# A two-layer decoder trunk on one core: the first embedding projection at the attention's end, squares on VectorE, weight low parts by an accumulating DMA

## The chip, the core and the metric

The kernel runs on one core of a Trainium2 chip. The metric is the device time of one execution, in microseconds (us); before the change the median of three runs is 1500.62 us (1500.09 to 1501.07). The core's engines run their own instruction queues: PE (TensorE, matrix products, with its weight loads as PEld), DVE (VectorE), ACT (ScalarE), POOL (GpSimd) and SP (SyncE, here an issuer of DMA). They meet only at semaphores: an instruction waits until the one that makes its input, or frees its buffer, is done. SBUF holds tiles of 128 partitions; PSUM takes what PE accumulates.

## The reference

512 tokens of width 1024 pass two layers: the first with differential attention, the second with retention. Each is followed by a squared-ReLU MLP and by a gated embedding.

```
for i in range(2):
    h = rms_norm(x, norm_mix[i])
    x = x + (diff_attention(h) if i % 2 == 0 else retention(h))
    h = rms_norm(x, norm_mlp[i])
    x = x + square(relu(h @ mlp_w1[i])) @ mlp_w2[i]
    gate = sigmoid(rms_norm(x, norm_pe[i]) @ pe_w_gate[i])
    x = x + gate * (p[i] @ pe_w_up[i])          # p[i]: 512 x 256
```

The product `p[i] @ pe_w_up[i]` depends on inputs alone and on nothing that the layer computes. Everything is float32.

## The kernel before

**Tiling.** Activations lie with features in partitions: x is eight tiles of 128 x 512, and so are the normalized z. A product of two float32 values is made from three matmuls of a shorter format (`mm3`, L177): each operand is split into a high part (a cast) and a low part (what the cast left off), and high x high, high x low and low x high are accumulated. Names end in h for the high and l for the low part: zh and zl, oT6h and oT6l, wh and wl.

**Weights.** The class `Weights` (L51) streams all weights in one order, in tiles of 128 x 1024 numbered from 0. For each, SP loads the raw tile (512 KB, three buffers), ACT casts it to wh (L75) and an engine subtracts to make wl (L79); wh and wl have five buffers each, so tile i reuses the buffer of tile i - 5, and tile i is prepared four tiles ahead of its use. `lo_engines` says who subtracts: DVE, and for the tiles prepared within the attention POOL and DVE by halves.

**Stages, by the span.** Attention to about 283 us, first MLP to 629, its gated embedding to about 690, retention to about 1083, second MLP to about 1430, second gated embedding to the end. In the attention, a plan of numbers (`place`) interleaves the steps of query and key projection, scores, softmax, values and the output product, and a scheduler then orders each engine's instructions by its own costs. The output product (`out_unit`) runs in groups of heads; group 2 (heads 6 and 7) is the last: for each of eight x tiles it adds the product to x (DVE, L516), then makes zh and zl for the MLP (`make_z`; ACT L159, DVE L160) and adds the squares of x to `acc` (`squares`; ACT L228, POOL L229). `acc` goes through a cast (rsm0sh), a subtraction (rsm0sl) and two matmuls against ones (rsm0p, `rs_rows`) to the row sums that the first MLP needs when its first two products are done.

**Order around the row sums.** The MLP's product functions run two output tiles side by side at the start (`tiles`, L193) and put the row sums' two matmuls (`late[0]`) at a fixed place in the second one, by default ahead of its third input tile (`late_at` 2).

**Embedding projection.** `up_unit` makes one 128 x 512 tile of `p @ pe_w_up` with six matmuls. In layer 0 it stands in the gated embedding, one tile ahead of each gate product (`begin`), with the two weight tiles `w_up0` loaded there; DVE multiplies it from PSUM. In layer 1 all eight tiles are made at the end of the retention, from two PSUM buffers (`ps_tr`), and ACT copies them to SBUF (pus, L797). PSUM has eight buffers: three `mm`, two `s`, two `tr`, one `av`.

## Time and profile before

| | |
|---|---|
| median of three runs | 1500.62 us |
| lowest, highest | 1500.09, 1501.07 us |
| the profiled execution | 1498.45 us |
| its span | 1496.6 us |
| PE busy | 98% of the span |
| DVE busy | 55% |
| ACT busy | 41% |
| POOL busy | 12% |

The profile is one execution. Its span is the time from its first to its last instruction, and 1.85 us lie around it. The page gives shares over the whole span, which averages stages with different limits; so a stage is read from windows (busy time of each engine in a stretch), and a single wait from the timeline, in which the brackets give the engine's idle time ahead of an instruction and what ended it. Matmuls overlap, so one's duration is longer than the distance to the next. The chain of waits follows the work that ended last backwards, and gives the share of each line in it.

### The profile page before, as it was taken

What the parts mean: (1) busy time and instruction counts of PE and PEld (TensorE: products, weight loads), DVE (VectorE), ACT (ScalarE), POOL (GpSimd) and SP (SyncE); (2) the same over time, 40 slices, a digit from 0 to 9 for tenths busy, and PEclk for the clock granted to TensorE, in tenths of its full rate; (3) what the DMA queues carried; (4) which work ended last, traced back from release to release, by engine and by line L of the source; (5) the groups of instructions that cost most, each with busy time, mean ns of one, the idle gap of its engine ahead of it and who ended that gap; (6) DMA issues with size and microseconds to landing.
All of it is one profiled execution on the core that took longest, in us unless ns stands there. A gap on an engine that the chain in (4) does not pass through costs nothing.

```text
span 1496.6 us, 17071 instructions
## 1 busy us (share of the span) xinstructions
PE 1470.9 (98%) x6668; PEld 1199.6 (80%) x6668; DVE 827.7 (55%) x1217; ACT 618.7 (41%) x966; POOL 183.6 (12%) x128
## 2 busy tenths in 40 slices
PE   9999999899999999999999999999999999999998
PEld 7667667688888888888888888888778888888887
DVE  7887888853434444475464564544584343434455
ACT  6666766541323224344442432433453241323332
POOL 4123223300000000311020110301220000000020
PEclk9999999999999999999999999999999999999999
DMA  6211131243333233232314233132233333333312
GB/s 234 61 57 57 57 113 57 81 116 99 98 92 95 96 99 99 85 99 93 105 51 132 64 99 106 57 127 71 71 99 99 98 94 93 96 98 99 99 57 85
DMA packets 40256, 137.90 MB, mean 92 GB/s; under 512 B 4464, under 2 KB 4976, under 8 KB 40176
## 3 DMA queue, kind: packets, MB, share of 16 engines
q1 hardware_dynamic: 40176, 136.82, 29.5%
q8 instruction: 52, 0.85, 0.2%
q14 instruction: 28, 0.23, 0.0%
HBM read 134.70 MB, written 2.10 MB: 91 GB/s over the span
## 4 chain that ended last, share of the span: by engine, by line
PE 88%; DVE 7%; ACT 2%; issue 1%; POOL 0%; DMA 0%; SPq 0%; POOLq 0%; DVEq 0%; ACTq 0%
PE py L179 8%; PE py L180 8%; PE py L181 8%; PE ph L180 8%; PE ph L181 8%; PE ph L179 8%; PE pg L181 2%; PE pg L180 2%; PE pg L179 2%; PE rv L180 2%; PE rqk L181 2%; PE rqk L180 2%; PE rv L181 2%; PE rv L179 2%; PE rqk L179 2%; PE rg L179 2%
## 5 line engine op out<-in xcount | busy, mean ns | idle before, releaser
L75 ACT CAST wh<-raw 128x1024 fp32r<-128x1024 f32 (+1 forms) x245 | 256.4, 1048 | 620.9 <-PE py L180 235.7
L79 DVE TENSOR_TENSOR wl<-raw,wh 128x1024 fp32r<-128x1024 f32 (+1 forms) x245 | 300.6, 1228 | 60.5 <-ACT wh L75 59.4
L180 PE MATMUL ph<-zl,wh 128*128 128x512 f32 x512 | 200.1, 391 | 3.5 <-DVE zl L160 3.4
L181 PE MATMUL ph<-zh,wl 128*128 128x512 f32 x512 | 199.8, 391 | 0.0
L179 PE MATMUL ph<-zh,wh 128*128 128x512 f32 x512 | 199.5, 390 | 0.1
L179 PE MATMUL py<-hh,wh 128*128 128x512 f32 x512 | 199.2, 389 | 0.0
L180 PE MATMUL py<-hl,wh 128*128 128x512 f32 x512 | 199.2, 389 | 0.0
L181 PE MATMUL py<-hh,wl 128*128 128x512 f32 x512 | 199.2, 389 | 0.0
L582 DVE TENSOR_TENSOR x<-x,py 128x512 f32<-128x512 f32 x64 | 44.0, 688 | 200.0 <-PE py L181 200.0
L572 DVE SCALAR_TENSOR_TENSOR ht<-ph,rsm 128x512 f32<-128x512 f32 x64 | 44.0, 691 | 158.8 <-PE ph L181 158.8
L180 PEld LDWEIGHTS ph<-zl,wh 128*128 128x128 f32 x512 | 96.5, 189 | 25.1 <-DVE zl L160 5.2
L179 PEld LDWEIGHTS ph<-zh,wh 128*128 128x128 f32 x512 | 96.4, 188 | 20.7 <-issue 0.5
L181 PEld LDWEIGHTS ph<-zh,wl 128*128 128x128 f32 x512 | 96.5, 189 | 20.1
L181 PEld LDWEIGHTS py<-hh,wl 128*128 128x128 f32 x512 | 96.1, 188 | 20.1
L179 PEld LDWEIGHTS py<-hh,wh 128*128 128x128 f32 x512 | 96.1, 188 | 20.0
L180 PEld LDWEIGHTS py<-hl,wh 128*128 128x128 f32 x512 | 96.1, 188 | 19.8
L229 POOL TENSOR_TENSOR acc_p<-acc_p,sq 128x512 f32<-128x512 f32 x14 | 24.2, 1727 | 673.7 <-ACT sq L228 673.7
L79 POOL TENSOR_TENSOR wl<-raw,wh 128x512 fp32r<-128x512 f32 x28 | 46.0, 1642 | 90.0 <-ACT wh L75 70.6
L179 PE MATMUL pqk<-wh,zh 128*128 128x512 f32 x128 | 53.6, 419 | 0.0
L179 PE MATMUL pg<-zh,wh 128*128 128x512 f32 (+1 forms) x136 | 51.2, 377 | 0.0
L181 PE MATMUL pg<-zh,wl 128*128 128x512 f32 (+1 forms) x136 | 51.2, 377 | 0.0
L180 PE MATMUL pg<-zl,wh 128*128 128x512 f32 (+1 forms) x136 | 51.2, 376 | 0.0
(874 smaller groups left out, 2762.9 us busy)
## 6 DMA issues: line engine op xcount, KB each, us to landing
raw<-in_w SPq DMA_DIRECT2D x128, 512.0 KB, 3.6
raw<-in_w_qk SPq DMA_DIRECT2D x16, 512.0 KB, 3.7
raw<-in_w_g SPq DMA_DIRECT2D x16, 512.0 KB, 3.6
raw<-in_w_rv SPq DMA_DIRECT2D x16, 512.0 KB, 3.7
raw<-in_w_rqk SPq DMA_DIRECT2D x16, 512.0 KB, 4.4
raw<-in_w_rg SPq DMA_DIRECT2D x16, 512.0 KB, 3.6
raw<-in_w_ro SPq DMA_DIRECT2D x16, 512.0 KB, 3.6
raw<-in_w_o SPq DMA_DIRECT2D x8, 512.0 KB, 3.6
```

What stands on the lines that cost most here:

```text
L75: nc.scalar.copy(out=hi[:, s], in_=raw[:, s])
L79: e.tensor_tensor(out=lo[:, r], in0=raw[:, r], in1=hi[:, r].bitcast(F32), op=ALU.subtract)
L179: nc.tensor.matmul(ps, a[0], b[0], start=start, stop=False)
L180: nc.tensor.matmul(ps, a[0], b[1], start=False, stop=False)
L181: nc.tensor.matmul(ps, a[1], b[0], start=False, stop=stop)
L229: nc.gpsimd.tensor_tensor(out=acc, in0=acc, in1=sq, op=ALU.add)
L572: nc.vector.scalar_tensor_tensor(out=t, in0=s[1], scalar=0.0, in1=rs, op0=ALU.max, op1=ALU.mult)
L582: nc.vector.tensor_tensor(out=x[m], in0=x[m], in1=ps, op=ALU.add)
```

## The change

The change has four parts.

1. **Low parts.** For the weight tiles 8 to 41 (`by_dma`), which are prepared from the attention's first scores until the first MLP's fifth tile, wl is no longer subtracted. ACT makes a second pass that writes -raw into wl, rounded as wh is, and a DMA issued by POOL adds the raw tile to it.
2. **First embedding projection.** `early_up` makes the eight tiles (pu0) among the units of the output product's group 2. The input p32, its two parts and the results lie in buffers of queries and keys that are dead by then (qh, ql, kl, kh). PSUM comes from `ps_tr` and `ps_s`. ACT copies each result (pus) and issues a DMA of 512 KB for each pair to DRAM (`up0`). In the gated embedding SP loads them back, one tile of 256 KB for each gate product. The order of weights follows.
3. **Squares at the attention's end** are added by DVE instead of POOL.
4. **Layer 1.** The row sums of the second MLP stand three input tiles later (`late_at` 5), and the second projection takes its PSUM from two pools by turns.

```diff
@@ class Weights, load
+        if self.by_dma:
+            self.tc.keep_in_program_order(nc.sync.dma_start(out=raw, in_=src))
+            nc.scalar.copy(out=hi, in_=raw)
+            nc.scalar.activation(out=lo, in_=raw, func=AF.Copy, scale=-1.0)
+            nc.gpsimd.dma_start(out=lo, in_=raw, accum_op=ALU.add)
+            self.made.append((hi, lo))
+            return
@@ order of weights
-    order += [w_o[i] for i in range(8)]
+    order += [w_o[i] for i in range(6)] + [w_up0[0], w_o[6], w_o[7], w_up0[1]]
...
-    order += gate_order(w_up0, w_g0)
+    order += [w_g0[i] for i in range(8)]
@@ squares
-    def squares(acc, src, k):
+    def squares(acc, src, k, engine=None):
...
-            nc.gpsimd.tensor_tensor(out=acc, in0=acc, in1=sq, op=ALU.add)
+            (engine or nc.gpsimd).tensor_tensor(out=acc, in0=acc, in1=sq, op=ALU.add)
@@ attention
-        W.lo_engines = (nc.gpsimd, nc.vector)
+        W.by_dma = True
...
-                    squares(st["acc"], x[m], m)
-
-        units = [(g, m, j) for g in range(2) for m in range(KD) for j in range(groups[g][1])]
-
-        units += [(2, m, j) for j in range(2) for m in range(4)]
-        units += [(2, m, j) for m in range(4, KD) for j in range(2)]
+                    squares(st["acc"], x[m], m, nc.vector)
+        def early_up(m):
+            if m == 0:
+                p32 = past("p32", "qh", F32)
+                load(p32, pT[0])
+                ph, pl = past("p0h", "ql", F32R), past("p0l", "kl", F32R)
+                split_into(ph, pl, p32)
+                pus["p"] = [cols((ph, pl), j) for j in range(2)]
+                pus["w"] = []
+            if m % 4 == 0:
+                pus["w"].append(W.next())
+            pu = (ps_tr if m % 2 == 0 else ps_s)(f"pu0{m}")
+            up_unit(pu, pus["w"], pus["p"], m)
+            if m % 2 == 0:
+                pus["t"] = past(f"pus{m}", ("kh", "kh", "qh", "ql")[m // 2], F32)
+            nc.scalar.copy(out=pus["t"][:, m % 2, :], in_=pu)
+            if m % 2 == 1:
+                nc.scalar.dma_start(out=up0[m // 2], in_=pus["t"])
+        units = [(out_unit, (g, m, j)) for g in range(2) for m in range(KD) for j in range(groups[g][1])]
+        units += [(early_up, (m,)) for m in range(0, 2)]
+        units += [(out_unit, (2, m, j)) for j in range(2) for m in range(4)]
+        units += [(early_up, (m,)) for m in range(2, 4)]
+        units += [(out_unit, (2, m, j)) for m in range(4, KD) for j in range(2)]
+        units += [(early_up, (m,)) for m in range(4, KD)]
...
-        W.lo_engines = (nc.vector,)
@@ mlp
+                    if (layer, c, f) == (0, 0, 4):
+                        W.by_dma = False
...
-                tiles(8, begin, unit, end, late if c == 0 else None)
+                tiles(8, begin, unit, end, late if c == 0 else None, late_at)
@@ gated embedding 0
+        def back(pool, m):
+            t = pool.tile([P, T], F32, name="put", tag="put", bufs=4)
+            load(t, up0[m // 2][:, m % 2, :])
+            return t
...
-            z, acc = gated_embedding(z, acc, p, 0, False, zslot)
+        z, acc = gated_embedding(z, acc, None, 0, False, zslot, made=back)
@@ layer 1
-                pu = ps_tr(f"pu1{m}")
+                pu = (ps_tr if m % 2 == 0 else ps_s)(f"pu1{m}")
...
-        z, acc = mlp(z, acc, 1)
+        z, acc = mlp(z, acc, 1, late_at=5)
```

How the instructions stand afterwards is shown at three places. In a row, L is the line (line numbers of the changed kernel are higher by 9 and more), then the operation, output<-inputs and the size; po is a tile of the output product (po17 the last of group 1, po20 to po27 those of group 2), pu0 a tile of the projection, ph000 and ph001 the first two products of the MLP.

On PE, at the end of the attention, the output product's group 2 began directly behind group 1:

```order
L180 MATMUL po17__2781<-oT5l_2561,wh29_2343 128x512
L181 MATMUL po17__2781<-oT5h_2560,wl29_2344 128x512
L179 MATMUL po20__2796<-oT6h_2715,wh30_2482 128x512
L180 MATMUL po20__2796<-oT6l_2716,wh30_2482 128x512
L181 MATMUL po20__2796<-oT6h_2715,wl30_2483 128x512
```

At that place there are now two units of the projection, whose first matmuls come ahead of it and the others after its first tiles:

```order
L189 MATMUL po17__2784<-oT5l_2564,wh29_2346 128x512
L190 MATMUL po17__2784<-oT5h_2563,wl29_2347 128x512
L188 MATMUL pu00_2805<-p0h_2794,wh30_2485 128x512
L188 MATMUL pu01_2814<-p0h_2794,wh30_2485 128x512
L188 MATMUL po20__2830<-oT6h_2718,wh31_2578 128x512
L189 MATMUL po20__2830<-oT6l_2719,wh31_2578 128x512
L190 MATMUL po20__2830<-oT6h_2718,wl31_2579 128x512
```

So the weight tile 30 is now one of the projection, and the output product's tiles are 31 and 32.

Further on, still on PE, the MLP followed the last unit of the output product:

```order
L180 MATMUL po27__2907<-oT7l_2743,wh31_2575 128x512
L181 MATMUL po27__2907<-oT7h_2742,wl31_2576 128x512
L179 MATMUL ph000_2949<-zh16_0_2817,wh32_2673 128x512
L180 MATMUL ph000_2949<-zl16_0_2818,wh32_2673 128x512
L181 MATMUL ph000_2949<-zh16_0_2817,wl32_2674 128x512
```

Now the last four units of the projection stand between them:

```order
L189 MATMUL po27__2959<-oT7l_2746,wh32_2676 128x512
L190 MATMUL po27__2959<-oT7h_2745,wl32_2677 128x512
L188 MATMUL pu04_2981<-p0h_2794,wh33_2754 128x512
L189 MATMUL pu04_2981<-p0l_2795,wh33_2754 128x512
L190 MATMUL pu04_2981<-p0h_2794,wl33_2755 128x512
```

In all, 48 matmuls more stand between the first of group 2 and the row sums rsm0p.

On ACT, at the same place, the weight casts stood between the zh (zh16) and squares (sq) of the x tiles:

```order
L75 CAST wh34_2790<-raw34_2789 128x1024
L156 CAST oT7h_2742<-osq_2694 128x512
L156 CAST p00h_2931<-p32_0_2929 128x512
L156 CAST p01h_2935<-p32_0_2929 128x512
L159 ACTIVATE zh16_0_2817<-x0_2281,sm_61 128x512
L75 CAST wh35_2856<-raw35_2855 128x1024
L225 ACTIVATE acc_0_2816<-x0_2281 128x512
L159 ACTIVATE zh16_1_2826<-x1_2331,sm_61 128x512
```

Now each weight has two passes, and the copies of results and their DMAs stand there too:

```order
L75 CAST wh34_2799<-raw34_2798 128x1024
L76 ACTIVATE wl34_2800<-raw34_2798 128x1024
L165 CAST oT7h_2745<-osq_2697 128x512
L561 COPY pus0_2812<-pu00_2805 128x512
L561 COPY pus0_2812<-pu01_2814 128x512
L563 DMA up0_181<-pus0_2812 128x1024
L168 ACTIVATE zh16_0_2851<-x0_2284,sm_61 128x512
L75 CAST wh35_2824<-raw35_2823 128x1024
L76 ACTIVATE wl35_2825<-raw35_2823 128x1024
L234 ACTIVATE acc_0_2850<-x0_2284 128x512
L168 ACTIVATE zh16_1_2860<-x1_2334,sm_61 128x512
L561 COPY pus2_2896<-pu02_2889 128x512
```

Behind the cast of tile 35 ACT has two more tiles with two passes each (36 and 37), six copies and three DMAs until it casts `acc` for the row sums.

On PE, at the start of the second MLP, the row sums rsm1p stood ahead of the third input tile (zh24_2):

```order
L181 MATMUL ph101_8738<-zh24_1_8595,wl173_8545 128x512
L237 MATMUL rsm1p_8766<-rsm1sh_8767,ones_r_67 128x512
L238 MATMUL rsm1p_8766<-rsm1sl_8768,ones_r_67 128x512
L179 MATMUL ph101_8738<-zh24_2_8606,wh173_8544 128x512
L180 MATMUL ph101_8738<-zl24_2_8607,wh173_8544 128x512
```

Now they stand behind the fifth:

```order
L188 MATMUL ph101_8771<-zh24_4_8677,wh173_8577 128x512
L189 MATMUL ph101_8771<-zl24_4_8678,wh173_8577 128x512
L190 MATMUL ph101_8771<-zh24_4_8677,wl173_8578 128x512
L246 MATMUL rsm1p_8808<-rsm1sh_8809,ones_r_67 128x512
L247 MATMUL rsm1p_8808<-rsm1sl_8810,ones_r_67 128x512
```

They moved nine matmuls back.


## Rows read from the trace of the kernel before

**Rows 1.** the page, part 1: busy us (share of the span) and instructions.

```profile
PE 1470.9 (98%) x6668; PEld 1199.6 (80%) x6668; DVE 827.7 (55%) x1217; ACT 618.7 (41%) x966; POOL 183.6 (12%) x128
```

**Rows 2.** windows: from:to us, length, busy us (x instructions) each, PEclk, DMA share, GB/s.

```profile
30.00:250.00 220.00, 210.77 (x1026) 155.93 (x1025) 178.95 (x490) 143.68 (x336) 59.41 (x46) 1.00 0.22 70
260.50:290.00 29.50, 23.64 (x90) 17.39 (x90) 24.71 (x28) 14.88 (x23) 13.95 (x10) 0.94 0.28 89
300.00:600.00 300.00, 300.00 (x1325) 248.43 (x1324) 128.13 (x145) 95.22 (x120) 1.05 (x1) 1.00 0.33 99
600.00:690.00 90.00, 90.00 (x399) 74.35 (x398) 53.11 (x61) 39.05 (x54) 20.85 (x14) 1.00 0.26 81
```

**Rows 3.** timeline of PE: start, us, instruction, count, [idle before it <-releaser].

```profile
260.56 0.39 PE L179 MATMUL po__2796<-oT6h,wh 128*128 128x512 f32 x1
...
264.21 0.51 PE L179 MATMUL po__2796<-oT7h,wh 128*128 128x512 f32 x1 [0.76 <-ACT oT7h L156]
...
273.12 0.50 PE L179 MATMUL po__2907<-oT6h,wh 128*128 128x512 f32 x1 [1.13 <-DVE x L516]
...
283.25 0.50 PE L180 MATMUL ph<-zl,wh 128*128 128x512 f32 x1 [3.38 <-DVE zl L160]
...
289.78 0.39 PE L238 MATMUL rsm0p<-rsm0sl,ones_r 128*128 128x512 f32 x1
```

**Rows 4.** tile views of acc and zl, 255 to 292 us: durations in ns.

```profile
L229 POOL TENSOR_TENSOR acc<-acc,sq x7: 1301/1590/1625, 270.5 to 281.1; 128x512 f32<-128x512 f32 x7
...
L160 DVE SCALAR_TENSOR_TENSOR zl<-x,sm,zh x8: 739/1168/1787, 268.2 to 284.9; 128x512 fp32r<-128x512 f32 x8
```

**Rows 5.** timelines of ACT at the two places, and of SP's issues.

```profile
274.58 1.05 ACT L75 CAST wh<-raw 128x1024 fp32r<-128x1024 f32 x1 [0.76 <-PE po__2907 L180]
275.53 0.63 ACT L228 ACTIVATE sq<-x 128x512 f32<-128x512 f32 x1
276.07 0.71 ACT L159 ACTIVATE zh<-x,sm 128x512 fp32r<-128x512 f32 x1
276.68 0.61 ACT L228 ACTIVATE sq<-x 128x512 f32<-128x512 f32 x1
...
1064.67 1.07 ACT L797 COPY pus<-pu 128x512 f32<-128x512 f32 x2
...
198.90 0.33 SPq L74 DMA_DIRECT2D raw<-in_w_o  x1
```

**Rows 6.** DMA issues (KB each, us to landing), and POOL's subtraction by tile.

```profile
raw<-in_w SPq DMA_DIRECT2D x128, 512.0 KB, 3.6
...
x<-in_xT SPq DMA_DIRECT2D x8, 256.0 KB, 3.0
...
L79 POOL TENSOR_TENSOR wl<-raw,wh x27: 1280/1752/1832, 33.0 to 261.7; 128x512 fp32r<-128x512 f32 x27
```

**Rows 7.** chain of waits, 30 to 250 us, share of 220 us by line.

```profile
by line: PE ps L414 10.9%; PE pqk L179 7.9%; PE pqk L181 7.4%; PE pqk L180 7.3%; issue 5.9%; DVE wl L79 3.5%; PE pt L437 3.3%; DVE es L425 3.1%; ACT wh L75 2.8%; PE pv L180 2.8%; PE pv L179 2.6%; PE pv L181 2.6%; DVE qkr L353 2.5%; PE ptqk 
```

**Rows 8.** timelines, weight tiles 11 and 23: ACT's cast, PE's first use of wl.

```profile
53.22 1.03 ACT L75 CAST wh<-raw 128x1024 fp32r<-128x1024 f32 x1
...
60.80 0.39 PE L180 MATMUL pqk<-wl,zh 128*128 128x512 f32 x1
...
161.99 1.05 ACT L75 CAST wh<-raw 128x1024 fp32r<-128x1024 f32 x1 [1.25 <-PE pqk L181]
...
170.60 0.39 PE L180 MATMUL pqk<-wl,zh 128*128 128x512 f32 x1
```

**Rows 9.** line 425, 30 to 250 us: durations in ns.

```profile
L425 DVE TENSOR_SCALAR es<-es,su,nlam x32: 336/478/1190, 47.4 to 232.8; 128x128 f32<-128x128 f32 x8, 128x256 f32<-128x256 f32 x8, 128x384 f32<-128x384 f32 x8, 128x512 f32<-128x512 f32 x8
```

**Rows 10.** timeline of PE, end of the retention and second MLP's row sums.

```profile
1065.31 0.50 PE L179 MATMUL pu<-p10h,wh 128*128 128x512 f32 x1 [1.49 <-ACT pus L797]
...
1104.57 0.50 PE L237 MATMUL rsm1p<-rsm1sh,ones_r 128*128 128x512 f32 x1 [1.89 <-ACT rsm1sh L156]
1105.30 0.50 PE L238 MATMUL rsm1p<-rsm1sl,ones_r 128*128 128x512 f32 x1 [0.23 <-DVE rsm1sl L157]
```

More of the change, by code (lines that the diff above doesn't have):

```diff
@@ L62, in __init__ @@
         self.parts = 1
+        self.by_dma = False
     def load(self):
@@ L291, in decoder_trunk, with up_unit @@
         squares(acc, t, k)
+    def up_unit(pu, wu, p, m):
+        for j in range(2):
+            o = (m % 4) * 256 + j * P
+            mm3(pu, cols(wu[m // 4], slice(o, o + P)), p[j], j == 0, j == 1)
+    dp = ctx.enter_context(tc.tile_pool(name="dp", bufs=1, space=bass.MemoryType.DRAM))
+    up0 = dp.tile([KD // 2, P, 2, T], F32, name="up0")
     with tc.tile_pool(name="at", bufs=1) as ap:
@@ L520, in out_unit, with past @@
                     zn.append(make_z(x[m], C_MLP, m))
-                    squares(st["acc"], x[m], m)
-        units = [(g, m, j) for g in range(2) for m in range(KD) for j in range(groups[g][1])]
-        units += [(2, m, j) for j in range(2) for m in range(4)]
-        units += [(2, m, j) for m in range(4, KD) for j in range(2)]
-        for u in units:
-            place(pos, out_unit, *u)
+                    squares(st["acc"], x[m], m, nc.vector)
+        pus = {}
+        def past(name, tag, dt):
+            return ap.tile([P, 2, T], dt, name=name, tag=tag, bufs=2)
+        def early_up(m):
[21 more added lines that the diff above has]
+        units += [(early_up, (m,)) for m in range(4, KD)]
+        for fn, u in units:
+            place(pos, fn, *u)
             pos += 1
@@ L554, in embedding, with mlp @@
         return [hilo(pl, f"p{layer}{j}", p32[:, j, :], tag=f"p{j}") for j in range(2)]
-    def mlp(z, acc, layer):
+    def mlp(z, acc, layer, late_at=2):
         late, rs = rs_rows(acc, f"rsm{layer}")
@@ L588, in mlp @@
         return zn, nacc
-    def up_unit(pu, wu, p, m):
-        for j in range(2):
-            o = (m % 4) * 256 + j * P
-            mm3(pu, cols(wu[m // 4], slice(o, o + P)), p[j], j == 0, j == 1)
     def gated_embedding(z, acc, p, layer, last, make=slot, made=None):
@@ L607, in begin @@
                 else:
-                    pu = made[m]
+                    pu = made(ap, m)
                 return W.next(), ps_mm(f"pg{layer}{m}") if whole(m) else None, pu
@@ L647, in zslot @@
             return zp.tile([P, T], dt, name=name, tag="z", bufs=16)
-        with tc.tile_pool(name="pl0", bufs=1) as pl:
-            p = embedding(pl, 0)
-            z, acc = mlp(z, acc, 0)
-            z, acc = gated_embedding(z, acc, p, 0, False, zslot)
+        def back(pool, m):
+            t = pool.tile([P, T], F32, name="put", tag="put", bufs=4)
+            load(t, up0[m // 2][:, m % 2, :])
+            return t
+        z, acc = mlp(z, acc, 0)
+        z, acc = gated_embedding(z, acc, None, 0, False, zslot, made=back)
         late, rs = rs_rows(acc, "rsr")
@@ L800, in decoder_trunk @@
             z = zn
-        z, acc = mlp(z, acc, 1)
-        gated_embedding(z, acc, None, 1, True, made=made)
+        z, acc = mlp(z, acc, 1, late_at=5)
+        gated_embedding(z, acc, None, 1, True, made=lambda pool, m: made[m])
 def _moving(w):
```

## The prediction

> **What bounds the kernel now.** I read first how busy each engine is over the span. TensorE (PE) is at 98% [rows 1], so only its idle time, about 26 us of 1496.6, and work taken off it can be gained. The second view cuts the span into stages. Between 300 and 600 us PE is busy all the time: 1325 matmuls in 300 us, 0.2264 us each, and between 600 and 690 us too (399 in 90 us, 0.2256). Two stretches have idle time. In the attention's body, 30 to 250 us, PE is busy 210.8 of 220 us beside a VectorE (DVE) at 179, and from 260.5 to 290 us it needs 29.5 us for 90 matmuls, which at 0.2264 are 20.4. So 9.1 us are lost at the attention's end, with the granted clock at 0.94 [rows 2].
>
> The timeline of PE there shows what it waited for. It idles 0.76 us for ScalarE's (ACT) cast oT7h, 1.13 us for DVE's residual addition and 3.38 us for a low part zl of DVE [rows 3]; the rest is short waits and the slower matmuls just behind the long one. The engines beside it: the seven additions of squares on POOL take 1.59 us each, and DVE's zl beside them take from 0.74 to 1.79 us, median 1.17 [rows 4]. So DVE and POOL slow each other, and PE pays. All ending times below are for the profiled execution, 1498.45 us (1.85 around its span); the median of the runs is 1500.62, 2.2 above it, and I add 2.2 at the end.
>
> **The change part by part.** *Embedding projection to the attention's end.* 8 tiles of 6 matmuls, 48, leave the gated embedding and enter the idle stretch. There they need 48 x 0.2264 = 10.9 us of PE, and the place they leave has no idle PE time [rows 2], so all 10.9 us go. What comes back is what the end grows by. If all 138 matmuls (90 + 48) run at full rate they take 31.2 us instead of 29.5: +1.7. Net **-9.1**, the lost time, provided that nothing else is late. Three sources are to be looked at.
> First, oT7: 25 matmuls stand between the start of the stretch and its first use instead of 9, so it is asked for 16 x 0.2264 = 3.6 us later, and PE idled for it 0.76 us. Second, DVE: it has seven additions more, but without POOL's beside it a zl costs nearer to the low end of 0.74 than to 1.17 [rows 4]. 8 zl save up to 8 x 0.43 = 3.4 us and the adds cost 7 x 0.74 = 5.2, and it has 10.9 us more before the first MLP matmuls. It is not late. Third, ACT. Its weight cast number 35 needs the buffer of tile 30, which the projection's fourth unit uses last, 48 matmuls after 260.56: 260.56 + 48 x 0.2264 + 0.39 = 271.8. From there ACT has by its order six weight passes, one first square, seven zh, seven squares, six copies of results and the cast of the sum of squares. By the spacing of rows a weight pass takes 0.95, a zh 0.61, a square 0.54 [rows 5], a copy 0.53 (half of the pair of 1.07), the first square the same: 5.7 + 0.5 + 4.3 + 3.8 + 3.2 + 0.6 = 18.1, so ready at 289.9. PE asks for it after 131 matmuls: 260.56 + 131 x 0.2264 = 290.2. Margin 0.3 us. ACT also issues the four result DMAs; no row shows an ACT issue, and the nearest is SP's, 0.33 us [rows 5]. Three of them lie in this chain: between 0 and 1.0 us. I take 1.0, since that row is a DMA issue of the same kind: **+0.7** (bounds 0 and 1.0). In the gated embedding the results come back by eight SP loads of 256 KB, each 3.0 us [rows 6] against 24 matmuls, 5.4 us, per tile: hidden. The load p32 stands on SP behind a weight load, and its cast on ACT ahead of oT6h: I cost it at nothing, because no matmul of the first unit stands ahead of the stretch; where the weight load ahead is late, oT6h is late by as much, which is part of D.
>
> *Low parts by accumulating DMA.* For 34 weight tiles the subtraction on POOL (half a tile, 1.75 us [rows 6]) and DVE (the other half) goes. ACT makes a second pass of about 1.05 us, and an accumulating DMA, issued by POOL, adds the raw tile. Of the chain of waits in the body 3.5% is DVE's subtraction and 2.8% ACT's cast [rows 7]: 7.7 and 6.2 us of 220. If the first goes and the second doubles, that gives **-1.5**. It could be -7.7 (second pass beside other work) or +6.2 (DVE's place in the chain taken by the next thing).
> How late can the low part come? No row shows an accumulating or POOL-issued DMA. A load of 512 KB lands in 3.6 us, one of 256 KB in 3.0, so 256 KB more cost 0.6 and the second source of 512 KB 1.2: 4.8. Before it stands POOL's part, between 0 and 1.75, the time POOL now needs for half a tile; I take 1.0: L = 5.8 us. Lower bound 3.6 (one load), upper 2 x 3.6 + 1.75 = 9.0 (two loads one after the other) [rows 6]. What there is: tile 11's cast begins at 53.22 and takes 1.03, the second pass 1.05, the first use of its low part is at 60.80: 5.5 us. Tile 23: 161.99, 1.05, 1.05, 170.60: 6.5 us [rows 8]. These are two of four blocks of query and key weights; in the other two the tightest tile, read in the same way, has 7.6. So at 5.8 one tile is late, by **+0.3**, and at the upper bound of 9.0 all four: 4 x 9.0 - 27.2 = 8.8 us. Behind the issue on POOL's queue are its small steps for the heads (osu, osq), which DVE waits for. An issue must wait for ACT's second pass, 1.05 us at most after the cast, and today POOL itself is busy for 1.75 there: no cost, down to a gain of 0.7 each that nothing late waits for.
>
> [...] The row first: DVE's es in the body, which reads and writes SBUF, takes 0.48 us at the median and 1.19 at most beside other work [rows 9]. [...]
>
> *Layer 1.* The second projection gets four PSUM buffers instead of two: the 1.49 us that PE waits for a copy at 1065.31 goes, -1.5 (the copies of 0.53 are faster than a unit of 6 x 0.2264 = 1.4). The row sums of the second MLP stand 9 matmuls, 2.04 us, later and were waited for 1.89 + 0.23 us [rows 10]: -2.0. Together **-3.5**; each bounded below by 0, if the order puts another wait there.
>
> Sum: -9.1 + 0.7 - 1.5 + 0.3 - 3.5 = -13.1. 1498.45 - 13.1 = 1485.35, and 2.2 above it **1487.5**.
>
> **The rivals.**
> *B, ACT has room.* ACT is busy 144 of 220 us in the body [rows 2], so the second passes hide and the accumulations land early: the body gives -7.7 and no lateness, the end no ACT wait. -9.1 - 7.7 - 3.5 = -20.3: 1480.3. For it speaks ACT's idle third, against it that ACT's cast is in the chain already.
> *C, ACT takes DVE's place.* ACT then is busy 144 + about 26 of 220 us, and its softmax steps stand behind passes of 1.05 us. The body loses 6.2 and repays nothing, the end waits the full 1.0: -9.1 + 1.0 + 6.2 + 0.3 - 3.5 = -5.1: 1495.5. For it: ACT's cast holds nearly as much of the chain as DVE's subtraction [rows 7].
> *D, slower: the low parts land late.* Place: the last weight tile of each of the body's four blocks, where PE has nothing else to run. With L above 7.6 each us costs four. Against the forecast's -13.1 - 0.3 = -13.4 it decides from 4L - 27.2 = 13.4, L = 10.2 us. My upper bound is 9.0; beyond it come one POOL step ahead in the queue (1.75) and one es of 1.19: 11.9, at which 20.4 are lost: 1498.45 - 13.4 + 20.4 + 2.2 = 1507.7. [...] Against it: it needs all three delays at each block.
> *E, the change doesn't reach its place:* the order shows that the 48 matmuls do stand there and rsm1p does stand later, so I give this nothing.
>
> **How the numbers follow.** Forecast with its bounds (L of 3.6 to 9.0): 50%, at 1484 to 1494. B 12%, C 25%, D 13%. The range goes from 1479 (B) to 1502, which leaves out most of D and a little below B. A measurement tells about 0.2%, 3 us, from no change: faster is below 1497.6, slower above 1503.6. Forecast and B, and most of C, are faster: 0.79; the rest of C and the mild part of D same: 0.09; slower 0.12.
>
> **What would show it.** Right: PE without a wait over 0.5 us from 260 to 290 us and 48 matmuls more there, the clock at 1.00; rsm0p waited for by ACT at most 1 us; the accumulating DMA landing about 5.8 us after issue; PE's waits for DVE in the body smaller, for ACT larger; 1065 and 1104 us without their waits. Wrong: waits of PE for wl or for the POOL queue's DMA at the end of each weight block (D); a longer body with ACT ahead of PE in the chain (C); body shorter by over 5 us (B). If POOL's issues alone take several us each, the forecast fails at L.

## The result

The changed kernel takes 1480.24 us (median of four runs, 1479.87 to 1481.67); the kernel before, run beside it, 1500.36 us. The ratio is 0.987, with a 95% interval of 0.9857 to 0.9882: 20 us, or 1.3%, faster. The profiled execution takes 1480.16 us, its span is 1478.0 us; before it was 1498.45 and 1496.6.

Part 1 of the page after, which answers to [rows 1]: the busy time of each engine over the span.

```profile
PE 1468.3 (99%) x6668; PEld 1199.8 (81%) x6668; DVE 787.4 (53%) x1189; ACT 650.6 (44%) x1007; POOL 157.9 (11%) x127
```

PE is busy nearly as long as before, 1468.3 us, with the same number of matmuls. What went is idle time. The windows after, with the columns of [rows 2], for the attention's body, for the attention's end (from the first matmul behind group 1 to the row sums) and for the gated embedding:

```profile
30.00:250.00 220.00, 217.54 (x1054) 160.95 (x1054) 153.97 (x471) 168.20 (x369) 45.28 (x48) 1.00 0.55 132
...
254.50:285.80 31.30, 31.30 (x137) 25.44 (x136) 20.47 (x31) 23.47 (x36) 4.07 (x5) 1.00 0.91 239
...
600.00:690.00 90.00, 90.00 (x402) 74.61 (x401) 57.02 (x66) 42.03 (x58) 20.94 (x14) 1.00 0.32 109
```

In the body PE ran 1054 matmuls in the 220 us in which it ran 1026 before: 28 more, or 28 x 0.2264 = 6.3 us of work that now fits in. DVE is busy 154 us there instead of 179, ACT 168 instead of 144. At the end there is no idle time left and the clock is at 1.00 (before: 23.64 busy of 29.5, and 0.94). The gated embedding has no idle time, as before, and 48 matmuls fewer to do.

The timeline of PE after, at the places of [rows 3] and [rows 10]: start, duration, instruction, and in brackets the idle time before it.

```profile
254.53 0.63 PE L188 MATMUL pu<-p0h,wh 128*128 128x512 f32 x2
...
285.36 0.39 PE L247 MATMUL rsm0p<-rsm0sl,ones_r 128*128 128x512 f32 x1
...
1045.77 0.40 PE L188 MATMUL pu<-p10h,wh 128*128 128x512 f32 x1
...
1087.62 0.50 PE L246 MATMUL rsm1p<-rsm1sh,ones_r 128*128 128x512 f32 x1
...
1088.34 0.50 PE L247 MATMUL rsm1p<-rsm1sl,ones_r 128*128 128x512 f32 x1 [0.23 <-DVE rsm1sl L166]
```

The stretch at the attention's end begins at 254.53 instead of 260.56 us; 131 matmuls later PE comes to the row sums and waits for nothing. The second projection at 1045.77 runs without the wait of 1.49 us, and of the waits of 1.89 and 0.23 us for the second MLP's row sums the first is gone.

Step by step, by the starts of the same matmuls in the two profiled executions:

| stage | forecast, us | measured, us |
|---|---|---|
| body (first query and key matmul to the end of group 1) | -1.5 + 0.3 = -1.2 | -6.5 |
| attention's end, with the projection taken out of the gated embedding | -9.1 + 0.7 = -8.4 | -8.9 |
| layer 1 | -3.5 | -4.1 |
| rest (start, tail) | 0 | +1.2 |
| profiled execution | -13.1 | -18.3 |

The body is 29.46 to 260.56 before and 29.92 to 254.53 after: 231.1 and 224.6 us. The row sums' second matmul to the retention's first row sums is 403.5 us before (289.78 to 693.28) and 393.0 after (285.36 to 678.36), so -10.5, while the stretch ahead grew from 29.2 to 30.8, +1.6: -8.9 in all. Second projection to second gated embedding is 393.2 before (1060.63 to 1453.84) and 389.1 after (1045.77 to 1434.86).

So the two stages that I had worked out from idle time came as forecast, and the body gained five times as much. The experiments ask why.

### The profile page after: what moved, and what is told of

The parts are those of the page before. It is cut to its first block, busy times and chain, and to the rows that moved or that the text cites. A ratio compares the mean times of both kernels' runs of the same rounds, so it can differ in the third digit from the quotient of the medians.

```text
span 1478.0 us, 17131 instructions
## 1 busy us (share of the span) xinstructions
PE 1468.3 (99%) x6668; PEld 1199.8 (81%) x6668; DVE 787.4 (53%) x1189; ACT 650.6 (44%) x1007; POOL 157.9 (11%) x127
## 4 chain that ended last, share of the span: by engine, by line
PE 94%; ACT 3%; DVE 2%; issue 1%; POOL 0%; DMA 0%; SPq 0%; POOLq 0%; ACTq 0%; DVEq 0%
PE py L190 8%; PE py L188 8%; PE py L189 8%; PE ph L188 8%; PE ph L190 8%; PE ph L189 8%; PE rg L188 2%; PE rg L189 2%; PE pg L188 2%; PE pg L189 2%; PE pg L190 2%; PE rv L188 2%; PE rv L190 2%; PE rqk L190 2%; PE rqk L188 2%; PE rv L189 2%
## 5 line engine op out<-in xcount | busy, mean ns | idle before, releaser
L84 ACT CAST wh<-raw 128x1024 fp32r<-128x1024 f32 (+1 forms) x211 | 221.0, 1049 | 603.0 <-PE py L189 235.7
L88 DVE TENSOR_TENSOR wl<-raw,wh 128x1024 fp32r<-128x1024 f32 (+1 forms) x211 | 267.2, 1267 | 54.6 <-ACT wh L84 53.3
L189 PEld LDWEIGHTS py<-hl,wh 128*128 128x128 f32 x512 | 96.1, 188 | 20.1
L190 PE MATMUL pqk<-wh,zl 128*128 128x512 f32 x128 | 51.5, 402 | 0.0
L189 PE MATMUL pqk<-wl,zh 128*128 128x512 f32 x128 | 51.4, 401 | 0.0
```

The lines of the kernel that those rows point to most:

```text
L84: nc.scalar.copy(out=hi[:, s], in_=raw[:, s])
L88: e.tensor_tensor(out=lo[:, r], in0=raw[:, r], in1=hi[:, r].bitcast(F32), op=ALU.subtract)
L189: nc.tensor.matmul(ps, a[0], b[1], start=False, stop=False)
L190: nc.tensor.matmul(ps, a[1], b[0], start=False, stop=stop)
```

## The experiments

The gain of a version is its difference to the kernel before that ran beside it on the same chip, since the medians of that kernel differ a little between chips (1499.3 to 1500.5). The changed kernel stands at -20.1 us.

| version | median, us | before beside it | gain | ratio, 95% interval |
|---|---|---|---|---|
| changed kernel | 1480.24 | 1500.36 | -20.1 | 0.9857 to 0.9882 |
| halves by POOL and DVE (part 1 undone) | 1486.45 | 1499.35 | -12.9 | 0.99 to 0.9927 |
| subtraction by DVE alone | 1483.29 | 1499.35 | -16.1 | 0.9879 to 0.9906 |
| ACT's second pass twice | 1496.77 | 1499.35 | -2.6 | 0.9971 to 0.9989 |
| accumulating DMA twice | 1541.98 | 1499.35 | +42.6 | 1.0269 to 1.0297 |
| before + part 1 alone | 1492.07 | 1500.45 | -8.4 | 0.9931 to 0.9958 |
| squares on POOL (part 3 undone) | 1479.70 | 1500.45 | -20.8 | 0.985 to 0.9877 |
| projection not moved (part 2 undone) | 1483.60 | 1500.45 | -16.9 | 0.9877 to 0.9904 |
| layer 1 undone (part 4) | 1486.20 | 1500.45 | -14.3 | 0.9891 to 0.9918 |
| no second pass on ACT | 1475.69 | 1499.26 | -23.6 | 0.9832 to 0.9859 |
| POOL kept busy | 1485.40 | 1499.26 | -13.9 | 0.9897 to 0.9924 |
| before, DVE alone subtracts | 1492.90 | 1499.26 | -6.4 | 0.9949 to 0.9974 |
| squares on POOL, osq parts on DVE | 1480.10 | 1499.26 | -19.2 | 0.9863 to 0.9894 |

### Where the body's time was: part 1 undone

```diff
-        W.by_dma = True
+        W.lo_engines = (nc.gpsimd, nc.vector)
...
+        W.lo_engines = (nc.vector,)
...
-                    if (layer, c, f) == (0, 0, 4):
-                        W.by_dma = False
```

> The changed kernel (1480.2 us) with its part 1 undone: the low parts are again subtracted by POOL and DVE in halves, all else stays. Theory (the attention's body gained 6.5 us because the subtraction left DVE, and because DVE's other steps no longer share with POOL's halves, while ACT's second passes hide): the body loses the 6.5 again, 1486 to 1489. Rival (the body gained by the new order of the instructions): 1480 to 1482.

By the gains it is 7.2 us slower than the changed kernel. The window of its body (columns as in [rows 2]):

```profile
30.00:250.00 220.00, 210.81 (x1025) 155.95 (x1025) 178.81 (x491) 144.20 (x337) 59.87 (x45) 1.00 0.23 73
```

PE runs 1025 matmuls there, one fewer than the kernel before [rows 2]. PE's waits in its body (engine, line and what it waited for; us in total, times, longest):

```profile
PE ptqk L404 <- DVE qkt L388: 1.9, 2, 1.6
PE pn L246 <- DVE aT0l L166: 1.7, 1, 1.7
PE pn L246 <- DVE kl L169: 1.5, 1, 1.5
```

The changed kernel's, same view and stretch:

```profile
PE pn L247 <- POOL osq1l L166: 0.6, 1, 0.6
PE ps L432 <- DVE mn L434: 0.6, 1, 0.6
PE ptqk L404 <- DVE qkt L388: 0.5, 1, 0.5
```

So the body's gain hangs on part 1, and the new order of instructions is not its cause: with the halves the waits for DVE's steps are back, 5.1 us in these three rows, which stand at the same 1.9, 1.7 and 1.5 us in the kernel before. But part 1 does three things at once: it takes a subtraction off DVE, it takes one off POOL, and it puts a pass on ACT. The next five runs take them apart.

### DVE alone subtracts

```diff
-        W.by_dma = True
...
-                    if (layer, c, f) == (0, 0, 4):
-                        W.by_dma = False
```

> The changed kernel with the low parts subtracted by DVE alone, whole tiles of 1.23 us: DVE has about 6 us more of its own work in the body than with halves, but POOL's halves no longer run beside it. If what counts is how long DVE's steps last beside POOL: most of the gain stays, 1481 to 1484. If what counts is the subtraction's own time on DVE: as with halves or worse, 1487 to 1491.

1483.29 us, the first of the two cases. The window of its body:

```profile
30.00:250.00 220.00, 216.10 (x1045) 159.29 (x1044) 179.39 (x494) 145.49 (x340) 20.87 (x23) 1.00 0.24 77
```

DVE is as busy as in the kernel before (179.4 us; there 178.95 [rows 2]), and yet PE runs 1045 matmuls here, 19 more than before and 9 fewer than in the changed kernel. What differs from before is POOL: 21 us busy instead of 59. DVE's busy time was not what held PE.

The same edit, made to the kernel before alone:

```diff
-        W.lo_engines = (nc.gpsimd, nc.vector)
```

> The kernel before with one line less: DVE alone subtracts in the attention, whole tiles. If POOL's halves beside DVE cost the body 5 of its 6.5 us: 1494 to 1497. If DVE's own subtraction counted: 1500 to 1504.

The window of its body:

```profile
30.00:250.00 220.00, 216.09 (x1042) 159.20 (x1041) 179.15 (x493) 145.76 (x341) 21.72 (x23) 1.00 0.24 73
```

It is 6.4 us faster than the kernel before, by leaving out one line, a little better than the first case had it. In the body it runs 1042 matmuls, 16 more (3.6 us); the rest of its gain lies at the attention's end, where POOL's last halves also ran: between 250 and 300 us it runs 197 matmuls instead of 180, PE waits 4.0 us instead of 5.7, and the clock is at 1.00 instead of 0.97.

### POOL kept busy beside DVE

```diff
+            nc.gpsimd.tensor_tensor(out=self.spare, in0=raw[:, 0:448], in1=hi[:, 0:448].bitcast(F32), op=ALU.subtract)
             nc.scalar.activation(out=lo, in_=raw, func=AF.Copy, scale=-1.0)
             nc.gpsimd.dma_start(out=lo, in_=raw, accum_op=ALU.add)
...
+    W.spare = gp.tile([P, 448], mybir.dt.bfloat16, name="spare")
```

> The changed kernel with a subtraction on POOL for each of the 34 tiles, written to a spare buffer that nobody reads (448 columns, about 1.4 us each): POOL works beside DVE as in the kernel before, but neither DVE nor PE depends on it. If what DVE loses beside POOL made up most of the body's 6.5 us: +3 to +5, 1483 to 1485. If only the subtraction's own time on DVE counted: 1480 to 1481.

The window of its body:

```profile
30.00:250.00 220.00, 212.82 (x1033) 157.15 (x1033) 158.53 (x467) 163.80 (x361) 69.21 (x70) 1.00 0.52 129
```

6.2 us of the gain are lost (-13.9 instead of -20.1), and 21 matmuls fewer run in the body than in the changed kernel, 4.8 us: the first case, and a little more. Nobody reads what POOL makes here, and PE waits for no wl. The longest waits of PE in the body are again those for qkt, aT0l and kl, as with part 1 undone:

```profile
PE ptqk L406 <- DVE qkt L390: 1.7, 2, 1.2
PE pn L247 <- DVE aT0l L167: 1.5, 1, 1.5
PE pn L247 <- DVE kl L170: 0.9, 1, 0.9
```

The price is paid in DVE's steps. Two of them in the body of the kernel before (least, median and largest ns), the multiplication qkt of 128 x 512 and the small step qku of 128 x 8:

```profile
L370 DVE TENSOR_TENSOR qkt<-qkt,qkr x16: 681/691/1828, 40.0 to 211.8; 128x512 f32<-128x512 f32 x16
...
L359 DVE TENSOR_TENSOR qku<-qky x16: 152/160/1254, 38.8 to 209.2; 128x8 f32<-128x8 f32 x16
```

In the changed kernel, the same two, and es, which answers to [rows 9] (1.19 us at most there):

```profile
L388 DVE TENSOR_TENSOR qkt<-qkt,qkr x16: 684/691/695, 39.9 to 206.7; 128x512 f32<-128x512 f32 x16
...
L377 DVE TENSOR_TENSOR qku<-qky x16: 157/167/170, 38.7 to 205.6; 128x8 f32<-128x8 f32 x16
...
L443 DVE TENSOR_SCALAR es<-es,su,nlam x32: 340/445/547, 47.6 to 226.7; 128x128 f32<-128x128 f32 x8, 128x256 f32<-128x256 f32 x8, 128x384 f32<-128x384 f32 x8, 128x512 f32<-128x512 f32 x8
```

A step of 128 x 8 elements takes 0.16 us at the median, with single ones of 1.25 before and at most 0.17 in the changed kernel; the multiplication's longest went from 1.83 to 0.70. The timelines show what the long ones stand beside. First the kernel before (a half of wl on POOL, es on DVE), then POOL kept busy (the added subtraction, a small step):

```profile
46.58 1.80 POOL L79 TENSOR_TENSOR wl<-raw,wh 128x512 fp32r<-128x512 f32 x1 [11.82 <-ACT wh L75]
47.41 1.04 DVE L425 TENSOR_SCALAR es<-es,su,nlam 128x128 f32<-128x128 f32 x1
...
60.10 1.19 POOL L76 TENSOR_TENSOR spare<-raw,wh 128x448 bf16<-128x448 f32 x1 [3.72 <-DVE qkr L374]
60.30 1.01 DVE L380 TENSOR_TENSOR qku<-qku,qkr 128x8 f32<-128x8 f32 x1
```

Both DVE steps end just behind POOL's instruction: es 0.07 us after it, the small step 0.02. In the body of the kernel before, 17 DVE steps last over 0.1 us longer than the shortest of their form while a POOL subtraction runs, 15.5 us together; 15 of them (13.3 us) stand beside a half of wl, and two beside a low part of the heads' squares (osq), which the change leaves on POOL. In the changed kernel no step is stretched so beside a subtraction. Nor was every step in the kernel before. Of the DVE steps that by their shortest time would have fitted inside one POOL subtraction of the kernel before (30 to 292 us), the 22 of qkt, qku, es, osq, wl and zl, which read and write SBUF alone, were all delayed, by 0.4 to 1.2 us; the 21 with an operand in PSUM (among them the residual additions to x and the low parts aT) kept their time within 0.03 us, and so did five reciprocals of 128 x 2 (0.16 to 0.17 us).

The delayed steps stand in chains of single instructions that PE's transposes and scores wait for. So in these runs a POOL subtraction beside DVE (1.28 to 1.83 us in the kernel before) held such a DVE step until it ended: es of 128 x 128 takes 0.34 us at the least and 1.04 here, the step of 0.16 us up to 1.25. It is delayed, not slowed in proportion. The timeline gives neither of the two steps above a wait, so the engines meet here without a semaphore between them; by what, no row tells.

### What the second pass costs ACT

```diff
-            nc.scalar.activation(out=lo, in_=raw, func=AF.Copy, scale=-1.0)
-            nc.gpsimd.dma_start(out=lo, in_=raw, accum_op=ALU.add)
+            nc.gpsimd.dma_start(out=lo, in_=raw.bitcast(F32R))
```

> The changed kernel without ACT's second pass: the DMA on POOL's queue copies raw into wl instead of adding it to -raw (the low parts of 34 tiles are then the raw values; the subtraction is left out). It prices the pass that the change put on ACT. If it hides (rival B's assumption): 1479 to 1480.5. If a pass on ACT is worth what the third one cost (14.8 us in the body for 27 passes): below 1472. In between, with the body's remaining waits of 2.2 us gone: 1477 to 1479.

The window of its body:

```profile
30.00:250.00 220.00, 219.02 (x1077) 165.35 (x1078) 160.03 (x479) 150.19 (x349) 36.78 (x50) 1.00 0.43 141
```

By the gains it is 3.5 us below the changed kernel, and 23 matmuls more run in its body, 5.2 us. The middle case was nearer than the one in which the pass hides, and even it was too small. The DMA is also a shorter one here, a copy instead of an addition (3.6 us to landing at the median, 5.4 in the changed kernel), so the pass and the longer transfer are priced together. That PE never waited for wl in the changed kernel's body (its three rows under part 1 undone are the longest of its five waits, and none is for wl) speaks for the pass. The other side, a third pass:

```diff
             nc.scalar.activation(out=lo, in_=raw, func=AF.Copy, scale=-1.0)
+            nc.scalar.activation(out=lo, in_=raw, func=AF.Copy, scale=-1.0)
```

> The changed kernel with ACT's second pass done twice for each of the 34 tiles (+1.05 us of ACT each, 27 of them in the body). If ACT's passes hide in the body (theory): at most +2 there, and up to 5 at the attention's end where six such passes stand ahead of the row sums: 1480 to 1487, with the body no longer than 2 us above. If an ACT pass lies on the path (rival C): +6 in the body alone, 1486 to 1492.

The window of its body:

```profile
30.00:250.00 220.00, 209.95 (x987) 152.19 (x986) 147.23 (x455) 176.81 (x372) 39.80 (x44) 0.99 0.50 123
```

17.5 us of the gain are lost, far more than either case had: 67 matmuls fewer than in the changed kernel run in the window, 15.2 us for the 28 us of passes that the body has more. Rival C's case came with the third pass, not the second. In the body the first pass more costs about 0.19 us each (5.2 us for 27, the longer transfer included), the next 0.56 (15.2 for 27). ACT was a cover nearly used up.

### How late the low parts may be

```diff
-            nc.scalar.activation(out=lo, in_=raw, func=AF.Copy, scale=-1.0)
+            nc.scalar.activation(out=lo, in_=raw, func=AF.Copy, scale=-2.0)
+            nc.gpsimd.dma_start(out=lo, in_=raw, accum_op=ALU.add)
             nc.gpsimd.dma_start(out=lo, in_=raw, accum_op=ALU.add)
```

> The changed kernel with two accumulating DMAs for each of the 34 tiles, one after the other (the pass writes -2 raw and raw is added twice, so the low parts of these tiles come out doubled): issue to the last landing goes from 5.5 to about 11 us. By the prediction's margins (5.5, 6.5, 7.6, 7.6 us) the last tiles of four blocks are late by 11 x 4 - 27.2 = 17 us: 1497. If the tiles are prepared earlier than those margins say: 1480 to 1484.

By the gains it is 62.7 us slower than the changed kernel, where I had 17 for it. The waits, for the stretch of the 34 tiles:

```profile
POOL wl L78 <- DMA wl<-raw: 143.3, 30, 8.6
...
PE pqk L190 <- DMA wl<-raw: 16.6, 5, 6.0
...
PE pv L190 <- DMA wl<-raw: 6.0, 2, 5.6
```

PE waits 22.6 us for landings at tiles of query, key and value weights: the wait of rival D, at its place. Behind them stands a mechanism that D didn't have. POOL's queue holds the second DMA of a tile until the first has landed, and the next tile's stand behind it. Its timeline for two tiles, the second DMA of each:

```profile
53.44 0.86 POOL L78 DMA_DIRECT2D wl<-raw  x1 [6.98 <-DMA wl<-raw]
...
61.18 0.86 POOL L78 DMA_DIRECT2D wl<-raw  x1 [5.99 <-DMA wl<-raw]
```

One tile passes every 7.7 us. A tile of 24 matmuls lasts 24 x 0.2264 = 5.4 us on PE, so where weight tiles follow each other the queue is the slower one and the four tiles ahead are used up; that is argued from these two figures. A third part is the clock: it is at 0.94 in the body of this run and 0.86 between 250 and 300 us. How the 62.7 us divide among the three is not shown.

### The attention's end

Part 3 undone:

```diff
-                    squares(st["acc"], x[m], m, nc.vector)
+                    squares(st["acc"], x[m], m)
```

> The changed kernel with the squares at the attention's end added by POOL again. If the 48 matmuls moved there cover what DVE and POOL take from each other: 1480 to 1481. If the slower zl and the additions of 1.6 us reach PE again: +2 to +4, 1482 to 1484.

1479.70 us: no difference that can be told from none. DVE's zl here, beside POOL's additions of 1.6 us, then zl in the changed kernel:

```profile
L169 DVE SCALAR_TENSOR_TENSOR zl<-x,sm,zh x8: 747/1242/1829, 263.6 to 278.2; 128x512 fp32r<-128x512 f32 x8
```

```profile
L169 DVE SCALAR_TENSOR_TENSOR zl<-x,sm,zh x8: 747/750/752, 263.9 to 278.3; 128x512 fp32r<-128x512 f32 x8
```

The contention is back in full (a zl up to 1.83 us, 0.75 without), and it costs nothing: PE waits for no zl, with 24 matmuls of the projection between the output product and the MLP's first use of one. What part 3 is worth without that cover no run shows.

Part 2 undone (the projection is back in the gated embedding, the order of weights as before):

```diff
-    order += [w_o[i] for i in range(6)] + [w_up0[0], w_o[6], w_o[7], w_up0[1]]
+    order += [w_o[i] for i in range(8)]
...
-        units += [(early_up, (m,)) for m in range(0, 2)]
-        units += [(early_up, (m,)) for m in range(2, 4)]
-        units += [(early_up, (m,)) for m in range(4, KD)]
...
-        z, acc = gated_embedding(z, acc, None, 0, False, zslot, made=back)
...
+            z, acc = gated_embedding(z, acc, p, 0, False, zslot)
```

> The changed kernel without its part 2: the first embedding projection stays in the gated embedding. If the 48 matmuls are what fills the lost 9 us: +7 to +9, 1487 to 1489. If the shorter work of DVE (parts 1 and 3) closes most of the waits at the end by itself: +2 to +5, 1482 to 1485.

By the gains 3.2 us slower than the changed kernel, so the second case. PE's waits between 250 and 300 us:

```profile
PE ph L188 <- DVE ht L615: 1.5, 1, 1.5
PE po__2799 L188 <- ACT oT7h L165: 0.8, 1, 0.8
PE ph L189 <- DVE zl L169: 0.3, 1, 0.3
```

The 3.38 us for zl [rows 3] are 0.3 here without any matmul moved, and the clock is at 1.00 (0.94 before [rows 2]). From the first matmul of group 2 (254.92) to the row sums' second (279.03) it takes 24.1 us for work of 20.2: 4 us lost instead of 9.1. So about 5 of the 9.1 us were repaid by the shorter work of DVE and POOL, and the projection filled the other 4. The kernel before with part 1 alone (the branch in `load` that part 1 needs comes with it):

```diff
-        W.lo_engines = (nc.gpsimd, nc.vector)
+        W.by_dma = True
...
```

> The kernel before (1500.4 us) with part 1 alone: the low parts of the tiles prepared from the attention's first scores to the first MLP's fifth tile come by the accumulating DMA, all else as before. Theory: the body gains its 6.5 us, and the end loses less because DVE and POOL have less to do there: 1490 to 1494. Rival (the body's gain needs the other parts): 1498 to 1500.

1492.07 us, 8.4 faster than before, the middle of the first range; its wait for zl at the end:

```profile
PE ph L189 <- DVE zl L169: 1.7, 3, 0.7
```

It is at 1.7 us in three pieces, instead of 3.38. The parts overlap: undone one by one they take 7.2 (part 1), 3.2 (part 2), nothing (part 3) and 5.8 (part 4) from the gain, 16.2 of 20.1 us. The rest is lost with none of them alone; that two of them would each have repaid it is the likely reading, and no run shows it.

### Layer 1

```diff
-                pu = (ps_tr if m % 2 == 0 else ps_s)(f"pu1{m}")
+                pu = ps_tr(f"pu1{m}")
...
-        z, acc = mlp(z, acc, 1, late_at=5)
+        z, acc = mlp(z, acc, 1)
```

> The changed kernel without its part 4 (second projection from two PSUM buffers, row sums of the second MLP at their old place). Theory: +4, since the two waits at the retention's end and at the row sums return: 1484 to 1484.5. Rival (they were covered by something else): 1480 to 1481.

By the gains 5.8 us slower, about 2 more than expected. The timeline of PE at the second MLP's row sums, and the window behind them:

```profile
1090.51 0.49 PE L246 MATMUL rsm1p<-rsm1sh,ones_r 128*128 128x512 f32 x1 [1.89 <-ACT rsm1sh L165]
1091.24 0.50 PE L247 MATMUL rsm1p<-rsm1sl,ones_r 128*128 128x512 f32 x1 [0.23 <-DVE rsm1sl L166]
...
1092.34 0.63 PE L190 MATMUL ph<-zh,wl 128*128 128x512 f32 x1
1092.76 0.63 PE L188 MATMUL ph<-zh,wh 128*128 128x512 f32 x1
```

```profile
1091.00:1098.00 7.00, 6.77 (x24) 5.40 (x24) 3.54 (x2) 2.19 (x3) 0.00 (x0) 0.76 0.08 33
```

The two waits are those of before, 1.89 and 0.23 us. Behind them the matmuls stand 0.43 us apart instead of 0.23 for 3.0 us (1091.91 to 1094.90), and the granted clock of the window is 0.76. In the profiled execution of the kernel before the same waits stand [rows 10], and the clock stays at 1.00. In that of the kernel before with part 1 alone they stand too, and it falls again. The windows behind them in these two:

```profile
1105.00:1112.00 7.00, 6.77 (x30) 5.55 (x30) 4.79 (x4) 3.52 (x4) 0.00 (x0) 1.00 0.10 40
...
1097.70:1104.70 7.00, 7.00 (x25) 5.56 (x24) 3.56 (x2) 2.17 (x4) 0.00 (x0) 0.76 0.00 0
```

In the kernel before with DVE alone subtracting, whose first wait there is 1.89 us as well, the window behind it (1098 to 1105 us) is at 0.80. So the wait costs 2 us in all four, and more where the clock falls: here nine matmuls behind it take 3.64 us (1091.58 to 1095.22), in the kernel before 2.07 (1105.64 to 1107.71), so 1.6 us. Of the four runs of this version three have a mean clock of 0.999 and 1486.2 to 1487.0 us, the fourth 1.000 and 1483.7.

### A try at more

In the body POOL still makes the low parts of the heads' squares (osq), eight subtractions of 1.3 to 1.8 us, and PE waited 0.6 us for one. They were given to DVE, and the squares at the end to POOL.

```diff
-                po[h] = po[h], sq, slots(f"osq{h}", sq, lo_engine=nc.gpsimd)
+                po[h] = po[h], sq, slots(f"osq{h}", sq)
...
-                    squares(st["acc"], x[m], m, nc.vector)
+                    squares(st["acc"], x[m], m)
```

> The changed kernel with the squares at the attention's end on POOL again (it was no slower) and with the low parts of the heads' squares (eight subtractions of 1.3 to 1.8 us on POOL, for one of which PE waits 0.6 us) made by DVE: in the body POOL then has only small steps. 1477 to 1479.5 if this takes away what PE still waits for in the body; 1480 to 1482 if DVE's eight additional steps take its place.

1480.10 us: the same time. PE no longer waits for POOL's osq, but its wait for DVE's mn went from 0.6 to 1.2 us, and the body runs 1053 matmuls instead of 1054: DVE's eight steps took the place of what POOL's had cost. No version that computes the reference beats the changed kernel by more than can be told from none.

## Why the prediction was right, and where its sizes were off

The direction and the range held: 1480.24 us lies in 1479 to 1502, near its lower end, 7.3 us below the forecast. Of these 5.2 are in the profiled execution (1485.35 forecast, 1480.16 measured) and 2.1 are the step to the median.

**The body was the term that was mis-sized.** The working there took 7.7 us of DVE's subtraction off the chain of waits and put 6.2 of ACT on. The ACT half was about right: leaving out the pass, with a shorter DMA, gives 5.2 us back in the body, and the chain after shows the pass, by line, at 3.1% of 220 us, 6.8 us:

```profile
by line: PE ps L432 12.5%; PE pqk L188 11.6%; PE pqk L189 11.3%; PE pqk L190 11.1%; ACT wl L76 3.1%; ACT wh L75 3.1%; PE ptqk L404 3.1%; PE pt L455 3.1%; issue 2.4%; PE pv L189 2.4%; PE pv L188 2.2%; PE po L188 2.1%; PE pv L190 2.0%; PE po 
```

PE itself waits for ACT nowhere in the body, where I had looked for larger waits of that kind: its five waits there are for DVE and POOL, and the pass stands further back in the chain. What the sum left out is POOL. I had read that DVE and POOL slow each other from zl at the attention's end [rows 4], and used it there alone, though POOL's 27 halves [rows 6] run beside DVE through the whole body. With POOL kept busy, the body loses 4.8 us. Two steps that follow each other divide the gain. Giving POOL's halves to DVE brings the kernel before 16 matmuls in the body, 3.6 us, though DVE then has more to subtract. Exchanging DVE's subtraction for the pass and the DMA brings 9 more in the changed kernel (1045 to 1054), 2.0 us. So the exchange, which the sum had at -1.5, came nearly as worked out, and the term that it put at nothing is POOL beside DVE. The chain by line can't show this: it books a delayed qku or qkt under its own name, not under the neighbour that delayed it. The row that could have told it was es in [rows 9], 0.48 at the median and 1.19 at most; I put the maximum into rival D's sum, as a delay of the DMA, and did not see in it the contention that the change takes away.

**Rival B gave the measured time almost to the tenth (1480.3), but not for its reason.** It assumed that ACT's passes hide. They don't: without them, and with the shorter DMA, the body gains another 5.2 us. That the figure agrees is luck.

**The landing was right.** Forecast 5.8 us, measured 5.4 at the median; DMA issues after, as in [rows 6]:

```profile
wl<-raw POOLq DMA_DIRECT2D x34, 512.0 KB, 5.4
```

The issue itself on POOL (ns, least, median, most) and all landings in the attention:

```profile
L77 POOL DMA_DIRECT2D wl<-raw x33: 852/865/1066, 35.9 to 295.2; - x33
...
DMA to landing us min/median/max: 4.5/5.5/7.6
```

The late tile of +0.3 did not come: PE waits for no wl. With DVE busy 154 of 220 us, the issues take 0.85 to 1.07 us, and the landings spread over 3.1 us without one that PE waited for. The es of 1.19 us in rival D's sum is a term that no run shows as a delay of the DMA: of POOL's 30 waits ahead of an issue (30 to 300 us) 23 end with ACT's second pass and none with an es. Rival D's mechanism is real, as the doubled DMA shows, but its price was built on lateness tile by tile, and the queue's pace came on top.

**The attention's end: right sum, partly wrong reason.** -8.9 against -8.4. PE has no wait there and the clock is at 1.00, as said. But I credited all 9.1 us to the 48 matmuls, with the shorter steps only named as no hindrance; alone, parts 1 and 3 repay about 5. And the +0.7 for ACT was not there. ACT's timeline after:

```profile
263.05 1.05 ACT L75 CAST wh<-raw 128x1024 fp32r<-128x1024 f32 x1 [0.40 <-PE po__2842 L189]
...
268.18 0.63 ACT L237 ACTIVATE sq<-x 128x512 f32<-128x512 f32 x1
268.31 0.33 ACTq L563 DMA_DIRECT2D up<-pus  x1
268.71 0.71 ACT L168 ACTIVATE zh<-x,sm 128x512 fp32r<-128x512 f32 x1
...
280.07 0.64 ACT L165 CAST rsm0sh<-acc 128x512 fp32r<-128x512 f32 x1
```

The cast of tile 35 waits for the output product's matmul (po__2842, the last user of tile 31) and not for the projection's fourth unit, as I had assumed from the buffers' turn; it starts 8.5 us after the stretch's start, not 11.2. And the DMA that ACT issues (ACTq, 0.33 us) lies beside its running square: the next zh starts 0.53 us after the square, the spacing of [rows 5]. The cast of the sum of squares ends at 280.7, 4 us before PE asks; I had it 0.7 late. (The bounds that the prediction gives this term, 0 and 1.0, don't fit its own margin of 0.3: the upper one is 0.7, and rival C's 1.0 is 0.3 too much.)

**Layer 1** came as forecast, -4.1 against -3.5.

**The step to the median.** I added 2.2 us because the median of before stands that far above its profiled execution. After the change the two agree (1480.24 and 1480.16). The layer-1 run and the two beside it explain it at least in part: a wait of 2 us at the second MLP's row sums is followed by a lower granted clock in some executions (0.76 and 0.80 in the windows behind it) and not in others (1.00). The profiled one of before was one without, and the change took the wait away. That the other runs of before differ for this reason is argued from their mean clocks (0.999 in the runs of 1497.8 to 1498.7 us, mostly 0.997 and 0.998 above), not shown window by window.

## What to carry to other kernels

Before you price work that leaves an engine by its own busy time, look for what it slows beside it: compare the least, median and largest duration of the same small step on the neighbour, in the whole stretch where both run, and look first at steps whose operands all lie in SBUF: here the 22 that were delayed were of that kind, and none of the 21 with an operand in PSUM was. The halves that POOL took over from DVE to relieve it cost more than they relieved, and giving them back to DVE, with the same busy time there, gained 6.4 us by itself. An engine at two thirds of its time is no cover to count on twice: ACT (144 of 220 us in the body before) took one more pass per tile for 0.19 us each, and the next for 0.56.

## What the runs showed of the hardware

- A DVE step of 128 x 8 elements takes 0.16 us at the median and up to 1.25 us beside a POOL subtraction, which it outlasts by 0.02 us; ACT's casts of weights do not change (medians of 1.05 and 1.04 us in the two kernels, none over 1.06), nor do the 21 DVE steps beside it that have an operand in PSUM (within 0.03 us).
- A 512 KB accumulating DMA within SBUF lands 5.4 us after its issue at the median (4.5 to 7.6 in the attention), a plain copy of that size 3.6; the issue itself takes 0.86 us on POOL.
- The same wait of 1.89 us at the same place was followed by a lower granted clock in the profiled executions of three versions (0.76, 0.76 and 0.80 over the 7 us behind it), and by 1.00 in that of the kernel before.
- A DMA issued by ACT takes 0.33 us in its queue, beside the running instruction: the next one starts 0.53 us after that one's start (0.54 without the DMA).
